# Transposes without a reader in three stages, 256-column token products in the last layer, and one pair of subtractions on another engine

## The chip, the core and the metric

The kernel runs on one core of a Trainium2 chip. The metric is the device time of one execution in microseconds (us); before the change it is 1029.0 us, the median of 3 runs (1028.3 to 1030.1). PE is TensorE, which multiplies matrices; PEld is its loading of the stationary operand, which runs beside the multiplications; DVE is VectorE, ACT is ScalarE, POOL is GpSimd, SP is the engine that issues most of the DMAs.

## The reference, cut to what matters

Two small transformer stacks run one after the other on x, 256 tokens by 1024 channels, in float32. Of the five stages the following is what the change touches:

```python
# first block: a gated mixer, then a feed-forward part
proj = einsum('bsd,dc->bsc', rmsnorm(x, norm_mix_g), w_in)      # 14 groups of 512 columns
...
x = x + einsum('bsd,de->bse', m, w_out)
z = relu(einsum('bsd,df->bsf', rmsnorm(x, norm_ff_g), w_ff1))   # 4096 columns
x = rmsnorm(x + einsum('bsf,fd->bsd', z * z, w_ff2), norm_final_g)
# second block: differential attention + conv_ffn, then latent attention + conv_ffn
u = h @ w_up                                                     # 2 * 2816 columns
c = causal depthwise conv of u + conv_b;  g, val = split(c, 2)
x = x + (silu(g) * val) @ w_down
# after the last conv_ffn: rms_norm(x, final_norm_g)
```

## The kernel before, in words

Every weight is used in two halves. A raw tile of 128 rows and 1024 columns (512 KB) comes from memory on SP's queue, ACT writes its upper half `hi` (L178), DVE the remainder `lo` (L179). Activations have such halves too, written by `halves` (L334 to L337: the upper by ACT, the lower by DVE or by POOL, as the caller asks). A product is then three matmuls in a row, `hi*xh`, `hi*xl`, `lo*xh` (`mm3`, L195); all of them are recorded on L193. `split_to` keeps the weights three units ahead of their use, and loads five raw tiles ahead of that.

`group` computes 512 output columns as four tiles of 128 columns by 256 tokens: for each of 8 values of k there are 4 tiles of 3 matmuls, that is 12 matmuls for a k and 96 for a group, and the moving operand has 256 columns (the tokens). Its argument `between` names functions that run after a given k. `rows` adds 2 to 4 k-tiles to all eight output tiles at once (24 matmuls for each k). The order of the program is the order of the steps; PE executes its matmuls in that order.

Some short work on PE stands between the groups. `stats` gives two functions: `one` sums squares by token (matmuls of 1 column, L295) and `two` spreads the result over the partitions (`bcast`, L320). `gating` in the mixer multiplies 128x128 blocks (L489). In the last conv_ffn alone, `turn_x` transposes the final x: four times, after k = 4, 5, 6 and 7 of group 1, it transposes four 128x128 blocks with the identity (L932). The attention stages transpose too (L761, L807, L1142).

The last conv_ffn writes its result with tokens on the partitions (`last_rows`): the stationary operand is a 128x128 block of the activations and the moving one is 512 columns of a weight, so that a pair of k-tiles is 2 token blocks by 2 halves by 2 k by 3 = 24 matmuls of 512 columns, 264 in all.

In the feed-forward part `z_evac(g)` takes a group of 512 columns from PSUM: scale (DVE, L331), squared relu (DVE, L614), `halves` with POOL for the lower half (L337), in two parts of two tiles. The first one, `z_evac(0)`, is issued after k = 3 of group 1, and the rows of the second matrix that need it come right behind group 1. The program order between 250 and 270 us is: group 0, `one`, k = 0 to 3 of group 1, `two`, `z_evac(0)`, k = 4 to 7 of group 1, `z_evac(1)`, the first rows.

Of the kernel before, what the change touches and what calls it, by code (L numbers as in the profile page):

```python
# [16 lines left out]
P = 128  # L17
T = 256
# [5 lines left out]
HID_T = 22  # L24
# [60 lines left out]
class Builder:  # L85
# [114 lines left out]
    def cols(self, banks, u, n, kk, stride, xh, xl, first, last, tiles=None):  # L200

        for c in tiles if tiles is not None else range(n):
            o = kk * stride + c * P
            self.mm3(banks[c // 2][:, c % 2, :], u.hi[:, o:o + P], u.lo[:, o:o + P], xh, xl,
                     first and c % 2 == 0, last)

    def group(self, units, banks, ncol, xh, xl, nk=KD, between=None, bank=None):

# [206 lines left out]
    def mixer(self):  # L415
        nc, a = self.nc, self.a
# [5 lines left out]
        one, two = self.stats(st)  # L422
# [95 lines left out]
                self.conv(bufs["y"][:, k, :], z[:, i, :], "conv_a", k, 8, None)  # L518
        self.step(r2)
        for j in range(4):  # L520
            self.group(g[4 + j], cb[j], 4, xh, xl, between={4: (lambda j=j: gating(j),)})
            self.step(lambda j=j: cx_evac(j))

        bb = [[], []]
# [75 lines left out]
    def ff(self):  # L600
        nc, a = self.nc, self.a
        w1 = self.weights(a["w_ff1"], 2048, 2)
        w2 = self.weights(a["w_ff2"], 2048, 2)
        xh, xl = lambda k: self.xh[:, k, :], lambda k: self.xl[:, k, :]
        st, z, fb, ob = {}, {}, [[] for _ in range(8)], []
        one, two = self.stats(st)

        def z_evac(g):
            z[g] = (self.b4([4, T], F32R), self.b4([4, T], F32R))
            for i in range(2):  # L610
                sl = slice(2 * i, 2 * i + 2)
                t = self.scaled(fb[g][i], st["r"])
                q = self.t2()
                nc.vector.scalar_tensor_tensor(out=q, in0=t, scalar=0.0, in1=t, op0=ALU.max,  # L614
                                               op1=ALU.mult)
                self.halves(q, z[g][0][:, sl, :], z[g][1][:, sl, :], nc.gpsimd)
        zh, zl = lambda k: z[k // 4][0][:, k % 4, :], lambda k: z[k // 4][1][:, k % 4, :]

        def final(pr, bank):
            if pr == 0:  # L620
                self.norm_in(lambda k: self.gg[:, k:k + 1], lambda k: self.par("g_fin", k))
                p = PAR_AT
                nc.vector.tensor_tensor(self.gg, self.par_sb[:, p["g_fin"]:p["g_fin"] + 8],
                                        self.par_sb[:, p["g_attn0"]:p["g_attn0"] + 8], op=ALU.mult)
            self.residual(pr, bank)
            self.norm_pair(pr)

        def second(g):
            ks = range(4 * g, 4 * g + 4)
            self.row_bank = self.at_bank  # L630
            if g < 7:
                self.rows(w2[4 * g:4 * g + 4], ob, ks, 0, FF_T - 1, zh, zl)
            else:
                self.rows(w2[4 * g:4 * g + 4], ob, ks, 0, FF_T - 1, zh, zl, final)
        for g in range(8):
            if g == 1:
                self.step(one)
            self.group(w1[4 * g:4 * g + 4], fb[g], 4, xh, xl,
                       between={3: (two, lambda: z_evac(0))} if g == 1 else None)
            if g:  # L640
                self.step(lambda g=g: z_evac(g))
                second(g - 1)
        second(7)
# [229 lines left out]
    def conv_ffn(self, i, final=None):  # L873
# [31 lines left out]
        for g in range(11):  # L905
            if g == 1:
                self.step(one)
            bt = {}
            if g == 1:
                bt[3] = (two, lambda: evac(0))  # L910
                if not final:
                    for k in range(4):
                        bt[4 + k] = (lambda k=k: self.turn_x(k // 2, k % 2),)
            self.group(wu[4 * g:4 * g + 4], ub[g], 4, xh, xl, between=bt)
            if g:
                self.step(lambda g=g: evac(g))
            if g >= 2:
                down(g - 2)
# [18 lines left out]
    def last_rows(self, units, banks, ks, xh, xl):  # L937

        def add(b, c):
            ps = banks[2 * b + c].rearrange("p a t -> p (a t)")  # L940
            for u, k in zip(units, ks):
                h, l = xh(k)[:, b * P:(b + 1) * P], xl(k)[:, b * P:(b + 1) * P]
                cs = slice(c * 512, c * 512 + 512)
                self.mm(ps, h, u.hi[:, cs], k == 0, False)
                self.mm(ps, h, u.lo[:, cs], False, False)
                self.mm(ps, l, u.hi[:, cs], False, k == HID_T - 1)

        def fn():
            if not banks:
                banks.extend(self.at_bank() for _ in range(4))  # L950
            for b in range(2):
                for c in range(2):
                    add(b, c)
                    if ks[-1] == HID_T - 1:
                        self.last_piece(b, c, banks[2 * b + c].rearrange("p a t -> p (a t)"))
        self.step(fn, *units)
# [360 lines left out]
```

## Time and profile before

| what | value |
|---|---|
| median of 3 runs | 1029.0 us (1028.3 to 1030.1) |
| profiled execution, its own time | 1023.16 us |
| its span, from the first to the last instruction | 1021.4 us |
| PE busy | 997.7 us, 98% of the span |
| PEld busy | 960.3 us, 94% |
| DVE busy | 745.1 us, 73% |
| ACT busy | 569.7 us, 56% |
| POOL busy | 175.0 us, 17% |
| granted TensorE clock, mean | 0.994 |

The time outside the span is 1.8 us. The profiled execution is one execution, and 5.8 us below the median. A matmul's recorded duration reaches into the next one's, so that its real pace is read from how many start in a stretch of time.

### The profile page before, as it was taken

How to read it: one execution, taken by the hardware profiler on the slowest of the kernel's cores; microseconds unless marked ns; L12 is line 12 of the kernel's file. 1: busy time of each engine (PE TensorE's matmuls, PEld its weight loads, DVE VectorE, ACT ScalarE, POOL GpSimd, SP SyncE). 2: the span in 40 equal slices, each digit the busy share in tenths (PEclk: the TensorE clock that was granted, in tenths of full speed). 3: DMA queues.
4: the chain of work that ended last, by engine and by line, in shares of the span. 5: the costliest groups of instructions: out<-in, count | busy, mean ns of one | idle time of the engine just before them, and what ended most of it. 6: DMA issues, size and time to landing. Idle time of an engine off the chain costs nothing.

```text
span 1021.4 us, 19659 instructions
## 1 busy us (share of the span) xinstructions
PE 997.7 (98%) x7940; PEld 960.3 (94%) x7940; DVE 745.1 (73%) x1124; ACT 569.7 (56%) x895; POOL 175.0 (17%) x121
## 2 busy tenths in 40 slices
PE   8999999999999999989899999999998999999996
PEld 7999999999999999978799999999987899999995
DVE  5667766567656665778868887777889988887774
ACT  6644454445444444846576665555686667655553
POOL 2101300002311221452102201010422121100001
PEclk9999999999999999999999999999999999999999
DMA  9675555554555555353345465555553435655531
GB/s 334 220 259 170 185 184 185 189 187 159 202 196 190 194 194 195 113 206 129 109 159 187 158 209 181 194 181 160 176 168 127 145 114 195 205 190 185 187 104 41
DMA packets 51067, 180.36 MB, mean 177 GB/s; under 512 B 5664, under 2 KB 6176, under 8 KB 50976
## 3 DMA queue, kind: packets, MB, share of 16 engines
q1 hardware_dynamic: 50688, 178.58, 51.9%
q8 instruction: 62, 1.02, 0.4%
q10 hardware_dynamic: 288, 0.52, 0.1%
q14 instruction: 29, 0.24, 0.1%
HBM read 178.04 MB, written 1.05 MB: 175 GB/s over the span
## 4 chain that ended last, share of the span: by engine, by line
PE 88%; DVE 3%; ACT 3%; issue 2%; POOL 2%; DMA 1%; SPq 0%; POOLq 0%; DVEq 0%; ACTq 0%
PE mm L193 60%; PE at L193 24%; DVE lo L179 1%; ACT hi L178 1%; POOL tiny L308 1%; POOL xg L697 1%; DMA raw<-in_w_in 1%; PE at L1119 1%; DVE t L870 1%; PE at L1142 1%; ACT b L741 0%; ACT t L1129 0%; POOL t L869 0%; PE at L489 0%; PE at L1118 0%
## 5 line engine op out<-in xcount | busy, mean ns | idle before, releaser
L193 PE MATMUL mm<-b,hi 128*128 128x256 f32 x3584 | 638.6, 280 | 1.1 <-DVE b L1031 0.8
L193 PEld LDWEIGHTS mm<-b,hi 128*128 128x128 f32 x3584 | 547.9, 188 | 5.1 <-issue 2.1
L179 DVE TENSOR_TENSOR lo<-raw,hi 128x1024 fp32r<-128x1024 f32 (+2 forms) x336 | 416.6, 1251 | 181.9 <-ACT hi L178 180.9
L178 ACT CAST hi<-raw 128x1024 fp32r<-128x1024 f32 (+2 forms) x337 | 345.4, 1037 | 301.5 <-PE mm L193 230.4
L193 PE MATMUL mm<-b,lo 128*128 128x256 f32 x1792 | 499.9, 279 | 0.0
L193 PEld LDWEIGHTS mm<-b,lo 128*128 128x128 f32 x1792 | 336.7, 188 | 0.7 <-issue 0.7
L193 PE MATMUL at<-b,hi 128*128 128x256 f32 x1088 | 190.9, 278 | 1.0 <-POOL b L337 1.0
L193 PEld LDWEIGHTS at<-b,hi 128*128 128x128 f32 x1088 | 165.0, 188 | 2.2 <-POOL b L337 1.2
L193 PE MATMUL at<-b,lo 128*128 128x256 f32 x544 | 151.0, 278 | 0.0
L193 PEld LDWEIGHTS at<-b,lo 128*128 128x128 f32 x544 | 102.0, 187 | 0.0
L894 POOL TENSOR_TENSOR t<-t,t 128x512 f32<-128x512 f32 x22 | 40.3, 1833 | 289.9 <-DVE t L597 251.4
L597 DVE SCALAR_TENSOR_TENSOR t<-t,par,t 128x254 f32<-128x254 f32 (+1 forms) x176 | 76.0, 485 | 11.6 <-ACT t L595 11.0
L280 POOL TENSOR_TENSOR t<-t,t 128x512 f32<-128x512 f32 x18 | 26.0, 1445 | 197.5 <-ACT t L279 196.9
L193 PE MATMUL at<-hi,b 128*128 128x512 f32 x176 | 56.7, 394 | 0.0
L336 ACT CAST b<-t 128x512 fp32r<-128x512 f32 x50 | 30.9, 621 | 43.1 <-POOL t L894 36.4
L331 DVE TENSOR_TENSOR t<-mm,rbc 128x512 f32<-128x512 f32 x76 | 51.6, 687 | 0.2
L337 POOL TENSOR_TENSOR b<-t,b 128x512 fp32r<-128x512 f32 x16 | 29.7, 1864 | 119.6 <-ACT b L336 119.6
L193 PE MATMUL mm<-hi,b 128*128 128x512 f32 x144 | 48.8, 411 | 1.1 <-ACT hi L178 1.1
L595 ACT ACTIVATE t<-t,par 128x256 f32<-128x256 f32 x88 | 46.0, 591 | 6.4 <-DVE t L331 6.4
L337 DVE TENSOR_TENSOR b<-t,b 128x512 fp32r<-128x512 f32 x34 | 24.2, 718 | 23.0 <-ACT b L336 23.0
L193 PEld LDWEIGHTS at<-hi,b 128*128 128x128 f32 x176 | 32.9, 187 | 7.7
L193 PEld LDWEIGHTS mm<-hi,b 128*128 128x128 f32 x144 | 27.8, 194 | 8.2 <-ACT hi L178 1.9
(181 smaller groups left out, 709.2 us busy)
## 6 DMA issues: line engine op xcount, KB each, us to landing
raw<-in_ffn_up SPq DMA_DIRECT2D x88, 512.0 KB, 4.8
raw<-in_w_ff SPq DMA_DIRECT2D x64, 512.0 KB, 4.5
raw<-in_w_in SPq DMA_DIRECT2D x55, 512.0 KB, 4.8
raw<-in_ffn_down SPq DMA_DIRECT2D x44, 512.0 KB, 4.1
raw<-in_da_qk SPq DMA_DIRECT2D x16, 512.0 KB, 4.8
raw<-in_w_proj_a SPq DMA_DIRECT2D x8, 512.0 KB, 4.1
raw<-in_w_proj_b SPq DMA_DIRECT2D x8, 512.0 KB, 3.7
raw<-in_w_out SPq DMA_DIRECT2D x8, 512.0 KB, 4.9
```

The lines of the kernel that those rows point to most:

```text
L178: self.last_hi = self.nc.scalar.copy(hi[:, sl], w[:, sl])
L179: (u.eng or self.nc.vector).tensor_tensor(lo[:, sl], w[:, sl], hi[:, sl].bitcast(F32), op=ALU.subtract)
L193: self.nc.tensor.matmul(out, lhsT, rhs, start=start, stop=stop, skip_group_check=True)
L280: nc.gpsimd.tensor_tensor(self.ss, self.ss, sq, op=ALU.add)
L308: self.nc.gpsimd.tensor_tensor(r, ms, self.mhalf[:, :n], op=ALU.pow)
L331: self.nc.vector.tensor_tensor(o, bank, self.over2(r), op=ALU.mult)
L336: self.nc.scalar.copy(hi, src)
L337: (eng or self.nc.vector).tensor_tensor(lo, src, hi.bitcast(F32), op=ALU.subtract)
L595: nc.scalar.activation(y, z, AF.Identity, scale=w[2], bias=bias)
L597: nc.vector.scalar_tensor_tensor(out=y[:, d:], in0=z[:, :T - d], scalar=w[2 - d], in1=y[:, d:], op0=ALU.mult, op1=ALU.add)
L697: nc.gpsimd.tensor_tensor(xp, xp, self.over2(st["rx"]), op=ALU.mult)
L894: nc.gpsimd.tensor_tensor(y[0], y[0], y[1], op=ALU.mult)
```

## The change

A new function `pulse` takes a bank of the pool `at` and transposes four 128x128 blocks of x into it; nothing reads the bank. It is called twice in each of three places: in the mixer after k = 5 and k = 6 of the fourth of the groups `cb`, in the feed-forward part after k = 4 and k = 5 of group 1, and in the first conv_ffn after k = 4 and k = 5 of group 1. `last_rows` splits each matmul of 512 columns into two of 256. The lower halves of `z_evac(0)` move from POOL to DVE.

```diff
+    def pulse(self):
+
+        ps = self.at_bank().rearrange("p a t -> p (a t)")
+        for i in range(4):
+            self.nc.tensor.transpose(ps[:, i * P:(i + 1) * P], self.x[:, i, 0:P], self.ident)
...
         for j in range(4):
-            self.group(g[4 + j], cb[j], 4, xh, xl, between={4: (lambda j=j: gating(j),)})
+            bt = {4: (lambda j=j: gating(j),)}
+            if j == 3:
+                bt[5] = bt[6] = (self.pulse,)
+            self.group(g[4 + j], cb[j], 4, xh, xl, between=bt)
...
-                self.halves(q, z[g][0][:, sl, :], z[g][1][:, sl, :], nc.gpsimd)
+                self.halves(q, z[g][0][:, sl, :], z[g][1][:, sl, :], nc.gpsimd if g else None)
...
             self.group(w1[4 * g:4 * g + 4], fb[g], 4, xh, xl,
-                       between={3: (two, lambda: z_evac(0))} if g == 1 else None)
+                       between={3: (two, lambda: z_evac(0)), 4: (self.pulse,), 5: (self.pulse,)}
+                       if g == 1 else None)
...
                 if not final:
                     for k in range(4):
                         bt[4 + k] = (lambda k=k: self.turn_x(k // 2, k % 2),)
+                else:
+                    bt[4] = bt[5] = (self.pulse,)
...
-                cs = slice(c * 512, c * 512 + 512)
-                self.mm(ps, h, u.hi[:, cs], k == 0, False)
-                self.mm(ps, h, u.lo[:, cs], False, False)
-                self.mm(ps, l, u.hi[:, cs], False, k == HID_T - 1)
+                for j in range(2):
+                    o = ps[:, j * T:(j + 1) * T]
+                    cs = slice(c * 512 + j * T, c * 512 + (j + 1) * T)
+                    self.mm(o, h, u.hi[:, cs], k == 0 and j == 0, False)
+                    self.mm(o, h, u.lo[:, cs], False, False)
+                    self.mm(o, l, u.hi[:, cs], False, k == HID_T - 1)
```

On PE, in the mixer, the first pulse stands between k = 5 and k = 6 of the fourth group `cb` (its banks are mm_1047 and mm_1048; a row is written as output, then moving operand, then stationary operand; xg holds x):

```order
 L193 MATMUL mm_1048<-b_17_129,hi_1003 128x256
 L193 MATMUL mm_1048<-b_16_128,lo_1004 128x256
+L211 MATMUL at_1144<-ident,xg 128x128 x4
 L193 MATMUL mm_1047<-b_16_128,hi_1043 128x256
 L193 MATMUL mm_1047<-b_17_129,hi_1043 128x256
```

Nothing is moved there; four transposes are put between two triples, and so it is at the five other places.

On PE, in the last conv_ffn, these are the first token products of the row pair that follows group 2, of the kernel before (at_10470 is one of four banks, hi and lo are halves of the activations, b_1542 holds the weight):

```order
L193 MATMUL at_10470<-hi_10347,b_1542_10179 128x512
L193 MATMUL at_10470<-lo_10348,b_1542_10179 128x512
L193 MATMUL at_10470<-hi_10347,b_1542_10179 128x512
L193 MATMUL at_10470<-hi_10377,b_1542_10179 128x512
L193 MATMUL at_10470<-lo_10378,b_1542_10179 128x512
```

and of the change:

```order
L193 MATMUL at_10500<-hi_10586,b_1566_10320 128x256
L193 MATMUL at_10500<-lo_10587,b_1566_10320 128x256
L193 MATMUL at_10500<-hi_10586,b_1566_10320 128x256 x2
L193 MATMUL at_10500<-lo_10587,b_1566_10320 128x256
L193 MATMUL at_10500<-hi_10586,b_1566_10320 128x256
L193 MATMUL at_10500<-hi_10616,b_1566_10320 128x256
```

Each matmul of 512 columns has become two of 256, and each block of the activations is loaded as the stationary operand twice as often.

On DVE, in the feed-forward part, this is `z_evac(0)` and what follows it, of the kernel before (mm_2784 and mm_2785 are the banks of group 0, mm_2916 is one of group 1):

```order
L331 TENSOR_TENSOR t_414_2978<-mm_2784,rbc_2974 128x512
L614 SCALAR_TENSOR_TENSOR t_415_2980<-t_414_2978 128x512
L331 TENSOR_TENSOR t_416_2984<-mm_2785,rbc_2974 128x512
L614 SCALAR_TENSOR_TENSOR t_417_2986<-t_416_2984 128x512
L179 TENSOR_TENSOR lo_3131<-raw_2942,hi_3130 128x1024
L331 TENSOR_TENSOR t_426_3052<-mm_2916,rbc_2974 128x512
```

and of the change (lines 6 to 9 further down; b_415 is the lower half of z):

```order
L337 TENSOR_TENSOR t_416_2988<-mm_2794,rbc_2984 128x512
L623 SCALAR_TENSOR_TENSOR t_417_2990<-t_416_2988 128x512
L337 TENSOR_TENSOR t_418_2994<-mm_2795,rbc_2984 128x512
L343 TENSOR_TENSOR b_415_2987<-t_417_2990,b_414_2986 128x512
L623 SCALAR_TENSOR_TENSOR t_419_2996<-t_418_2994 128x512
L179 TENSOR_TENSOR lo_3151<-raw_2952,hi_3150 128x1024
L343 TENSOR_TENSOR b_415_2987<-t_419_2996,b_414_2986 128x512
L337 TENSOR_TENSOR t_430_3072<-mm_2926,rbc_2984 128x512
```

The two subtractions L343 stand in DVE's queue, each behind a result of ACT that it waits for, and ahead of a weight's lower half and of `z_evac(1)`.

## Rows read from the trace of the kernel before

**Rows 1.** The page's head, its PE row and the granted clock in 40 slices.

```profile
span 1021.4 us, 19659 instructions
PE 997.7 (98%) x7940; PEld 960.3 (94%) x7940; DVE 745.1 (73%) x1124; ACT 569.7 (56%) x895; POOL 175.0 (17%) x121
PEclk9999999999999999999999999999999999999999
```

**Rows 2.** L193 on PE by stretches: start:end, length, busy (matmuls), clock, DMA.

```profile
101.13:252.12 150.99, 150.99 (x1284) 1.00 0.54 180
265.92:417.90 151.98, 151.98 (x1343) 1.00 0.56 187
520.40:522.99 2.59, 2.59 (x24) 1.00 0.80 283
530.89:549.70 18.81, 18.81 (x168) 1.00 0.39 127
550.39:555.80 5.41, 5.41 (x48) 1.00 0.96 331
558.60:734.32 175.72, 175.72 (x1494) 1.00 0.53 176
850.77:861.43 10.66, 10.66 (x97) 1.00 0.30 91
867.02:878.32 11.30, 11.30 (x97) 1.00 0.58 181
985.37:996.67 11.30, 11.30 (x97) 1.00 0.01 1
```

**Rows 3.** Timeline of PE at the first turn_x: start, length, engine, line, tiles, count.

```profile
844.57 0.28 PE L193 MATMUL mm<-b,lo 128*128 128x256 f32 x1
844.68 0.60 PE L932 MATMUL at<-ident,xg 128*128 128x128 f32 x4
845.04 0.48 PE L193 MATMUL mm<-b,hi 128*128 128x256 f32 x2
845.35 0.28 PE L193 MATMUL mm<-b,lo 128*128 128x256 f32 x1
```

**Rows 4.** L932 by form: shortest, median and longest duration in ns.

```profile
L932 PE MATMUL at<-ident,xg x16: 271/272/273, 844.7 to 850.4; 128*128 128x128 f32 x16
```

**Rows 5.** Timeline of PE, two other short pieces: attention's transposes, conv_ffn's sums.

```profile
519.51 0.82 PE L761 MATMUL at<-ident,b 128*128 128x128 f32 x6
...
549.70 0.50 PE L295 MATMUL at<-ones,t 128*128 128x1 f32 x4
```

**Rows 6.** Timeline of PE where the feed-forward part's first rows begin.

```profile
264.19 0.28 PE L193 MATMUL mm<-b,lo 128*128 128x256 f32 x1
264.30 0.28 PE L193 MATMUL at<-b,hi 128*128 128x256 f32 x1
265.59 0.38 PE L193 MATMUL at<-b,hi 128*128 128x256 f32 x1 [1.00 <-POOL b L337]
```

**Rows 7.** Timelines of DVE, ACT and POOL around z_evac(0).

```profile
261.24 0.69 DVE L614 SCALAR_TENSOR_TENSOR t<-t 128x512 f32<-128x512 f32 x1
263.18 1.22 DVE L179 TENSOR_TENSOR lo<-raw,hi 128x1024 fp32r<-128x1024 f32 x1
...
262.56 1.35 ACT L336 CAST b<-t 128x512 fp32r<-128x512 f32 x2
...
263.25 6.23 POOL L337 TENSOR_TENSOR b<-t,b 128x512 fp32r<-128x512 f32 x3 [9.65 <-ACT b L336]
```

**Rows 8.** L193 on PE by stretches of 512-column matmuls alone, columns as above.

```profile
878.32:883.93 5.61, 5.61 (x27) 1.00 0.91 314
417.90:429.09 11.19, 11.19 (x50) 1.00 0.27 88
```

**Rows 9.** All engines by stretches: PE, PEld, DVE, ACT, POOL busy, then clock and DMA.

```profile
265.92:417.90 151.98, 151.98 (x1343) 151.98 (x1342) 93.27 (x89) 70.63 (x84) 29.63 (x17) 1.00 0.56 187
558.60:734.32 175.72, 175.72 (x1495) 175.72 (x1494) 136.19 (x195) 103.71 (x143) 32.60 (x17) 1.00 0.53 176
867.02:996.67 129.65, 129.65 (x937) 121.86 (x936) 103.51 (x134) 71.44 (x92) 10.39 (x8) 1.00 0.53 174
```

## The prediction

> **What bounds the kernel now.** I read the head of the page first: PE is busy for 997.7 of 1021.4 us at a granted clock of 0.9 or more in every slice [rows 1]. So PE is the bound nearly everywhere, and the question is not who makes it wait but how fast its matmuls follow one another. A matmul's duration can't tell that, since it overlaps the next; the count of starts can. So the second view is that of L193 on PE by stretches, with the 256-column matmuls alone [rows 2]. A count there includes one to three matmuls that only reach over an edge; in the long stretches this is nothing. The mixer from 101.13 us: 1282 starts in 150.99 us, 117.8 ns each. The feed-forward part from 265.92 us: 1341 starts in 151.98 us, 113.3 ns each. The first conv_ffn from 558.60: 1492 in 175.72 us, 117.8 again. The operation, its shape and the granted clock (1.00, so the upper of the two levels, 2.4 GHz) are the same in all three. There are two paces, 4.45 ns apart, and a stretch keeps its pace for up to 1500 matmuls.
>
> **What switches the pace.** The changes of pace that I found in the rows all lie at an interruption of the stream. Feed-forward: PE waits 1.00 us for POOL, 264.30 to 265.59 [rows 6], and the fast pace begins behind that wait; it goes on through the 512-column matmuls at 417.90. Last conv_ffn: four transposes at 844.68 [rows 3]; triples start 0.35 us apart before them, 0.34 after, and from 850.77 the rows show 94 in 10.66 us, 113.4 each [rows 2]. Then come the first 512-column products, and from 867.02 on each group of 96 takes 11.30 us, 117.7 each, up to the last at 985.37 [rows 2]. Not every interruption helps: after six transposes in the attention at 519.51 [rows 5] the pace stays slow (22 in 2.59 us from 520.40), and the sums by token at 549.70 [rows 5] turn a fast stream (166 in 18.81 us before) into a slow one (46 in 5.41 us after) [rows 2]. I read this as two stable spacings between the load of the stationary operand and the matmul behind it: an interruption draws one, and an undisturbed stream keeps it. That is an inference; the paces themselves are rows.
>
> **The pulses: price.** A pulse is turn_x without its copy, so its price is a row. From the `lo` at 844.57 to the `lo` at 845.35 are 0.78 us, with three matmuls and four transposes; three matmuls alone take 0.35. A pulse costs 0.43 us, 109 ns a transpose, and six cost 2.6 us [rows 3]. The record of one transpose is 272 ns long [rows 4], but four end to end start 0.36 us before the next matmul, so most of it overlaps. The Trainium skill, "TensorE: Matmul & The Clock Gate", section "Part 4: PE-mode transpose", puts a transpose at about 275 ns in one kernel's context; that is the recorded duration here, and 24 of them would by that estimate cost 6.6 us in place of 2.6. The trace's starts decide, so I take 2.6. Nothing reads the banks and x, the identity and the banks are long ready, so a pulse should wait for nothing; the banks that it takes from the pool of four were emptied before.
>
> **The pulses: what they bring, if the pace becomes the fast one.** Mixer: 1284 matmuls of 256 columns stand between the last gating and the next sums (36 of the fourth group, eleven groups' worth 1056, 192 of rows), 1260 of them behind the second pulse: 1260 x 4.45 = 5.6 us, less 0.9 for two pulses, 4.7 us. First conv_ffn: 48 of group 1, nine groups (864), 528 of rows and 72 of the next stage, less the 24 ahead of the second pulse: 1488 x 4.45 = 6.6, less 0.9, 5.7 us. Feed-forward: it runs fast already in this execution, so the pulses bring 24 x 4.45 = 0.1 us and cost 0.9.
>
> **z_evac(0) on DVE.** The wait of 1.00 us costs 1.29 - 0.12 = 1.17 us from start to start [rows 6]. What was late is POOL's lower half: 263.25 to about 265.1, one third of 6.23 us [rows 7]. On DVE it takes 0.7 (the like-sized L614, 0.69) behind ACT's upper half, which is ready at 263.2, so about 264.0. PE reaches the rows 0.9 us later than before because of the pulses, at 265.1. The wait goes: 1.2 us gained, and feed-forward comes to 1.2 + 0.1 - 0.9 = 0.4 us. Next in line is DVE itself: it gets 1.4 us more work, and stands 0.6 us or so at ACT's result, ahead of a weight half that ended at 264.4 and would end near 266 [rows 7]. The rows use it one k later, 265.1 + 2.7 = 267.8, so it is covered; the half behind `z_evac(1)` has less cover, an estimated 0.6 us from the same durations. If that is wrong PE waits up to 1 us; I take none.
>
> **256-column token products.** At 512 columns the price is 5.61 us for 24, 233.8 ns, and 11.19 for 48, 233.1 [rows 8]: 233.3. Two of 256 cost 226.7 at the fast pace and 235.6 at the slow one, so 264 of them bring 1.8 us or cost 0.6. What matters more is what stands between them: after the four turn_x the stream is fast and the 512-column products end that [rows 2]. Without them the eight groups from 867.02 on would stay fast: 768 x 4.45 = 3.4 us. Together 5.2 us. Twice as many loads of the stationary operand fit: every 256-column stream in the kernel has one for each matmul.
>
> A rule speaks against this edit. The Trainium skill, same page, section "Back-to-back issue gap", makes an isolated matmul N / 2.4 + 2.5 ns at the full clock, by which 256 columns take 109.2 and 512 take 215.8: one pace alone, and two halves would cost 2.5 ns more than the whole, 264 x 2.5 = 0.7 us lost. The rows differ from it at both widths (113.3 or 117.8, and 233.3).
>
> **Sum.** 4.7 + 0.4 + 5.7 + 5.2 = 16.0 us off the profiled execution's 1023.2: 1007.2. Its 1023.2 is 5.8 us below the median of 1029.0. One reading: in the timed runs the wait on POOL left feed-forward at the slow pace, 1341 x 4.45 = 6.0 us more. With that the pulses there gain these 6.0 too and the timed result is 1007. The other: the 5.8 us have another cause and stay, 1013. The trace can't decide, and I put down 1010, between them.
>
> **Can the others follow?** At 4% more pace DVE goes from 136.2 of 175.7 us (78%) to 81% in the first conv_ffn, from 103.5 of 129.7 (80%) to 83% in the last; ACT and the DMAs stand lower, and feed-forward has kept the fast pace at the same weight traffic with 187 GB/s [rows 9].
>
> **Rivals.**
> (1) One of mixer, first conv_ffn or last conv_ffn does not turn or stay fast. For: the transposes at 519.51 did not turn the pace, and the token form has never been seen at 256 columns. It costs back 5.6 to 6.6 us (5.8 in the last): 1013 by the profile, up to 1019 with the median's offset. Chance 0.27.
> (2) Two or more fail: 1019 to 1025. Chance 0.12.
> (3) Slower: a pulse leaves the pace as it is, and the wait whose end made feed-forward fast is gone. The pulses cost 2.6 us, the end of the wait gives 1.2, the token halves at the slow pace cost 0.6, and feed-forward loses its 6.0: 1023.2 + 8.0 = 1031.2, 2.2 over the median (and 1037 if the median's 5.8 have another cause). It decides where fewer than about 450 matmuls gain the fast pace, since the edits cost 2.0 us net without it (2.0 / 0.00445). Against it: the four turn_x at 844.68 are the same four transposes behind the same 12 matmuls after the same `bcast` as in the first conv_ffn, and the pace turned there [rows 3]. Chance 0.08. By the one pace for each width in the skill's section the pulses would be mere cost too; the two paces of the rows speak against that.
> (4) The pace turns but DVE or the weights can't follow, waits appear and undo the pace: 1014 to 1020. Against it [rows 9]. Chance 0.08.
> The forecast has 0.45.
>
> **Range and chances.** Both readings of the median and case (1) reach from 1005 to 1019; (2) adds 1025 with small weight. 1004 to 1021 leaves out less than 2 in 10. The likeliest case alone is 1005 to 1014. About 0.2% (2 us) is what a measurement of this kernel can tell from no change. Faster: the forecast, (1), (2), (4) less a little, 0.87; same 0.06; slower 0.07, from (3).
>
> **What would show it.** L193 by stretches: the mixer behind the second pulse, feed-forward, first conv_ffn and all groups of the last at 113.3 ns; a stage at 117.8 is a pulse that failed. Each pulse at 0.43 us. No wait of PE for POOL before the first rows, and none for DVE soon after. I am wrong if the stages stay at 117.8, if they lose the pace half way, or if the timed runs differ from the profile by more than 6 us.

## The result, and the profile after

The kernel with the change takes **1014.46 us** (median of 4 runs, 1012.61 to 1015.79); the kernel before took 1028.65 beside it (4 runs, 1023.5 to 1030.1). The ratio on record is 0.9884, 95% interval 0.9845 to 0.9923 (the two medians alone give 0.9862). The forecast was 1010.0 with a range of 1004 to 1021. The profiled execution of the change is the one of 1012.61 us, 10.6 below the profiled execution of before.

The page's head, its PE row and the granted clock of the change, which answer to [rows 1]:

```profile
span 1010.8 us, 20230 instructions
PE 986.3 (98%) x8228; PEld 961.3 (95%) x8228; DVE 745.2 (74%) x1126; ACT 568.9 (56%) x895; POOL 169.7 (17%) x119
PEclk9999999999999999999999999999999999999999
```

PE has 288 matmuls more and is busy 11.4 us less; its share of the span is the same 98%. PE was the bound and still is, and its work got shorter though there is more of it. Where, the count of starts tells. L193 on PE by stretches of the change, columns as in [rows 2]:

```profile
104.39:247.28 142.89, 142.89 (x1260) 1.00 0.57 185
257.39:412.52 155.13, 155.13 (x1368) 1.00 0.57 187
554.66:723.39 168.73, 168.73 (x1488) 1.00 0.56 181
757.34:761.38 4.04, 1.49 (x9) 0.58 0.39 116
841.20:852.16 10.96, 10.96 (x96) 1.00 0.31 98
852.16:869.36 17.20, 17.20 (x148) 1.00 0.64 210
869.36:885.46 16.10, 16.10 (x144) 1.00 0.70 222
885.46:902.55 17.09, 17.09 (x148) 1.00 0.58 193
985.36:1002.48 17.12, 17.12 (x146) 1.00 0.01 1
```

The first three rows are the stages behind the pulses of the mixer, the feed-forward part and the first conv_ffn: 142.89 / 1260, 155.13 / 1368 and 168.73 / 1488 are 113.4 ns each. The mixer and the first conv_ffn ran at 117.8 before [rows 2]. The rows from 841.20 on are the last conv_ffn, and there the pace is not what was forecast: fast for its first 96 matmuls, then slow for 146, fast for 142 to 144, slow again, and so to the end (a row's count takes in two or three matmuls that only reach over an edge; starts alone give 117.85 ns where it is slow and 113.36 where it is fast). Every piece begins at the first token products of a pair and ends ahead of the next pair's. The pace changes at all nine steps from a group to token products, and at none of the eight steps from token products back to a group.

The same from stage to stage, as the time to the end of each in the profiled executions, before and after: sums of the mixer 252.12 and 247.28 (-4.84); end of feed-forward's rows 417.90 and 412.52 (-0.54 more); sums of the attention 549.70 and 544.55 (+0.23); sums of the first conv_ffn 734.32 and 723.39 (-5.78); end of the latent attention 836.74 and 827.47 (+1.66); end of the span 1021.37 and 1010.82 (-1.28). Together -10.55.

The +0.23 of the attention hides two terms that nearly cancel: about 350 of its matmuls ran at 113.3 ns before and at 117.8 in the change (+1.6), and only the profile before has a piece at the lower clock there, which is the row at 453.36 below (-1.5: from the end of the wait ahead of it, the first 20 matmuls take 3.81 us before and 2.27 in the change).

The +1.66 is the row at 757.34: a granted clock of 0.58 in 4.04 us, which is a piece at the lower of the two levels, 1.2 GHz. PE had waited 1.74 us for DVE just ahead of it. In the profile of before the same thing lies elsewhere, at 453.36, behind a wait of 2.2 us of PE for DVE:

```profile
453.36:456.77 3.41, 3.41 (x17) 0.50 0.73 253
```

17 matmuls in 3.41 us would take about 2.0 at 117.8 ns each. Over the 14 profiles of this study there are none to two such pieces in the body of the kernel, all behind one of three waits of PE in the two attention stages. The wait of 1.74 us stands in all 14 (the profile before has it too, 1.75 us ahead of 768.14, and no lower clock behind it), and ten have a piece behind it. The kernel of the change, run again below, has the piece at 437 us that this profile lacks. So I take these pieces for no part of the change; that the change doesn't make the one at 757 us likelier is not shown, since the three profiles without 256-column token products all lack it.

### The profile page after: what moved, and what is told of

Same layout as the page of the kernel before. It is cut to its first block, busy times and chain, and to the rows that moved or that the text cites. A ratio compares the mean times of both kernels' runs of the same rounds, so it can differ in the third digit from the quotient of the medians.

```text
span 1010.8 us, 20230 instructions
## 1 busy us (share of the span) xinstructions
PE 986.3 (98%) x8228; PEld 961.3 (95%) x8228; DVE 745.2 (74%) x1126; ACT 568.9 (56%) x895; POOL 169.7 (17%) x119
## 4 chain that ended last, share of the span: by engine, by line
PE 86%; DVE 4%; ACT 3%; POOL 3%; issue 2%; DMA 1%; SPq 0%; POOLq 0%; DVEq 0%; ACTq 0%
PE mm L193 58%; PE at L193 24%; DMA raw<-in_w_in 1%; DVE lo L179 1%; DVE t L880 1%; ACT hi L178 1%; PE at L1133 1%; POOL tiny L314 1%; POOL xg L707 1%; ACT b L751 1%; PE at L1156 1%; POOL t L879 1%; POOL t L286 0%; ACT t L1143 0%; PE at L495 0%
## 5 line engine op out<-in xcount | busy, mean ns | idle before, releaser
L193 PE MATMUL mm<-b,hi 128*128 128x256 f32 x3584 | 629.3, 279 | 1.1 <-DVE b L1045 0.8
L193 PEld LDWEIGHTS mm<-b,hi 128*128 128x128 f32 x3584 | 543.7, 188 | 4.0 <-issue 1.8
L193 PE MATMUL mm<-b,lo 128*128 128x256 f32 x1792 | 497.9, 278 | 0.0
L193 PEld LDWEIGHTS mm<-b,lo 128*128 128x128 f32 x1792 | 336.4, 188 | 0.7 <-issue 0.7
L193 PE MATMUL at<-b,hi 128*128 128x256 f32 x1088 | 187.5, 277 | 0.0
L193 PEld LDWEIGHTS at<-b,hi 128*128 128x128 f32 x1088 | 164.1, 188 | 1.1 <-issue 1.0
L193 PE MATMUL at<-b,lo 128*128 128x256 f32 x544 | 150.4, 276 | 0.0
L193 PEld LDWEIGHTS at<-b,lo 128*128 128x128 f32 x544 | 102.2, 188 | 0.0
L193 PE MATMUL at<-hi,b 128*128 128x256 f32 x352 | 62.9, 279 | 0.0
L193 PEld LDWEIGHTS at<-hi,b 128*128 128x128 f32 x352 | 54.5, 189 | 0.0
L193 PE MATMUL at<-lo,b 128*128 128x256 f32 x176 | 49.2, 279 | 0.0
L193 PE MATMUL mm<-hi,b 128*128 128x512 f32 x144 | 47.6, 402 | 1.6 <-ACT hi L178 1.6
L343 POOL TENSOR_TENSOR b<-t,b 128x512 fp32r<-128x512 f32 x14 | 25.8, 1840 | 123.0 <-ACT b L342 123.0
L343 DVE TENSOR_TENSOR b<-t,b 128x512 fp32r<-128x512 f32 x36 | 25.6, 716 | 22.9 <-ACT b L342 22.8
```

The lines of the kernel that those rows point to most:

```text
L193: self.nc.tensor.matmul(out, lhsT, rhs, start=start, stop=stop, skip_group_check=True)
L343: (eng or self.nc.vector).tensor_tensor(lo, src, hi.bitcast(F32), op=ALU.subtract)
```

## The experiments

Four theories were to be told apart: (T) four transposes in a row turn the pace of the matmuls behind them, and that is the gain; (R1) the gain comes from the 256-column tokens or from the lower halves on DVE; (R2) any interruption or any extra work would do; (R3) a pulse draws the pace at random.

**The three parts alone.** The kernel before with the pulses only, with the 256-column tokens only, and with the lower halves on DVE only.

```diff
 e1 = before +   def pulse(self): ...
                 bt[5] = bt[6] = (self.pulse,)          (mixer, j == 3)
                 4: (self.pulse,), 5: (self.pulse,)     (feed-forward, g == 1)
                 bt[4] = bt[5] = (self.pulse,)          (conv_ffn, final)
 e2 = before +   for j in range(2): ... self.mm(o, h, u.hi[:, cs], k == 0 and j == 0, False)
 e3 = before +   self.halves(q, ..., nc.gpsimd if g else None)
```

> The kernel before with the six pulses alone; the last layer's products stay at 512 columns, POOL keeps the lower halves. Theory (a pulse turns the stream to the spacing of 113.3 ns, which then lasts): mixer behind the pulses, feed-forward and first conv_ffn at 113.3 to 113.4 ns a matmul, last conv_ffn at 117.8 as before; 10 to 11 us under a profile of the kernel before whose feed-forward is fast, that is 1011 to 1014 us in the profile and about the same in the timed runs. Rival (the time came from the other two edits): no stage but feed-forward differs from before, and six pulses cost 2.6 us: 1025 to 1032.

Measured: 1013.18 us (4 runs, 1011.01 to 1018.3) against 1028.75 of before (19 runs, 1027.38 to 1031.86), ratio 0.9856, interval 0.9826 to 0.9886. L193 by stretches in e1, the mixer, feed-forward and the first conv_ffn behind their pulses:

```profile
104.50:247.50 143.00, 142.80 (x1261) 1.00 0.55 185
257.50:412.00 154.50, 154.50 (x1365) 1.00 0.55 187
554.00:722.00 168.00, 168.00 (x1485) 1.00 0.54 180
```

The three stages run at the fast pace, the groups of the last conv_ffn at the slow one as before, and from the last turn_x to the last matmul PE takes 162.81 us, to the hundredth what it took before. POOL still writes the lower halves of `z_evac(0)` here, and PE doesn't wait for them: from the sums of the mixer to the end of feed-forward's rows e1 takes 165.23 us, the change 165.24.

> The kernel before with the 256-column token products alone. In the profile of the change the last conv_ffn changed its pace at the first token product of each row pair, from fast to slow and from slow to fast by turns. Theory (the step from a group to token products switches the spacing, whatever stands ahead of the last layer): the same alternation, about 145 matmuls at 117.8 and 143 at 113.4, and the last conv_ffn is 1.5 to 2.5 us shorter than before. Rival (the alternation comes from how the stream arrives from the earlier stages): one pace throughout, a gain of 5.2 us or a loss of 0.6.

Measured: 1028.24 us (10 runs), ratio 0.9994, interval 0.9982 to 1.0006. The alternation is the same as in the whole change, with a turn at each of the nine steps to token products, 161.04 us from the last turn_x to the last matmul and 8.62 us behind it; the feed-forward part ran at the slow pace in the profile.

> The kernel before with the lower halves of the first z on DVE alone. Theory (the wait of 1.0 us for POOL is what turned feed-forward to the fast spacing): without the wait feed-forward stays at 117.8 ns, so it gives 1.2 us and loses 6.0: 1027 to 1029 in the profile. Rival (feed-forward is fast for another reason, for example its shapes): 113.3 without the wait and 1021 to 1023.

Measured: 1028.25 us (10 runs), ratio 0.9998, interval 0.9987 to 1.0009. PE no longer waits for POOL ahead of feed-forward's rows.

What follows: the pulses bring everything that can be measured; R1 is out. The profiles of e2 and e3 also bear on the 5.8 us between the profile of before and its median. Timeline of PE in e2, where the first rows of feed-forward begin, and L193 by stretches behind it:

```profile
264.09 0.28 PE L193 MATMUL at<-b,hi 128*128 128x256 f32 x1
265.38 0.38 PE L193 MATMUL at<-b,hi 128*128 128x256 f32 x1 [1.01 <-POOL b L337]
...
266.06:422.00 155.94, 155.94 (x1326) 1.00 0.55 181
```

L193 by stretches in e3, which has no wait there:

```profile
259.06:420.00 160.94, 160.94 (x1369) 1.00 0.54 184
```

The wait of e2 is that of [rows 6], 1.01 us in place of 1.00, and behind it stand 155.94 / 1326 = 117.6 ns (117.8 by starts alone; so it is with each 117.6 below): the slow pace, where the profile of before had 113.3. So the same wait left one pace in one execution and the other in another. Without the wait (e3) the stage is slow too, 117.6. Of the 48 times of the kernel before that stand beside the change and these runs, five lie between 1022.0 and 1024.3 (four of them among the seven beside e5 to e8) and one at 1025.3, all others at 1027.4 or more. The profile of before, at 1023.16, is one of the low ones; that the low times are those with a fast feed-forward part is inferred from the two profiles, since no other time of that kernel was profiled.

**One pulse in place of two** in each stage, to see whether the second does anything.

```diff
-                bt[5] = bt[6] = (self.pulse,)
+                bt[5] = (self.pulse,)
```

> The change with the first pulse of each stage alone. Theory (the first pulse already turns the spacing, the second only keeps it): all three stages at 113.3 ns, 3 x 0.43 = 1.3 us less than the change: 1011.3 in a profile like that of the change, 1013 median. Rival (two are needed, or each is a draw): at least one stage at 117.8, 5 to 6 us more for each.

Measured: 1014.62 us (4 runs, 1010.12 to 1015.73), ratio 0.9855, interval 0.9829 to 0.988. One pulse turned feed-forward and the first conv_ffn; in the mixer it failed. L193 by stretches, the mixer of e4:

```profile
102.61:252.30 149.69, 149.69 (x1272) 1.00 0.54 180
```

That is 117.7 each. A pulse in the mixer can fail (R3 for this stage), and since two pulses fail there too in runs below, e4 doesn't show that two are needed.

**Is it the transposes?** Four plain matmuls of the same operands in the place of the four transposes (the identity and x change sides, without the transpose mode), and one transpose in the place of four; both twice in each stage.

```diff
-            self.nc.tensor.transpose(ps[:, i * P:(i + 1) * P], self.x[:, i, 0:P], self.ident)
+            self.nc.tensor.matmul(ps[:, i * P:(i + 1) * P], self.ident, self.x[:, i, 0:P],
+                                  start=True, stop=True)                              (e5)
-        for i in range(4):
+        for i in range(1):                                                             (e6)
```

> The change with each pulse's four transposes replaced by four plain float32 matmuls of the same blocks (same reads, same bank, about 0.9 us a pulse from the gating's 8 records at 0.11). Theory (a transpose sets the spacing, an ordinary short product does not: behind the gating's plain products the stream was slow four times of four): the three stages stay at 117.8 ns. Rival (any interruption of this kind turns it): they run at 113.3 as in the change.

Measured: 1032.14 us, one run (the kernel before beside e5 to e8: median 1024.27, 7 runs, 1021.99 to 1031.1). L193 by stretches, the three stages of e5:

```profile
105.50:253.50 148.00, 148.00 (x1259) 1.00 0.55 179
265.00:420.00 155.00, 155.00 (x1318) 1.00 0.57 184
568.00:736.00 168.00, 168.00 (x1429) 1.00 0.55 179
```

All three at 117.6: an interruption of 0.9 us (each plain matmul leaves two records, eight for a pulse) turned nothing. The edit changes the kind of the pulse and its length at once, and the last experiment shows that the length alone can matter; plain matmuls in another number were not tried.

> The change with one transpose in each pulse in place of four. Theory (the spacing after the transposes decides, and one has it already): 113.3 ns in the three stages, and a pulse costs about 0.1 us. Rival (it takes several in a row to settle): at least two stages at 117.8, as behind single transposes in the latent attention before.

Measured: 1022.13 us, one run. L193 by stretches in e6, and the one row of its timeline that tells why the second stage is fast all the same:

```profile
105.20:253.50 148.30, 148.24 (x1259) 1.00 0.55 180
266.44:420.00 153.56, 153.56 (x1349) 1.00 0.56 186
560.20:736.00 175.80, 175.60 (x1492) 1.00 0.55 176
...
266.21 0.19 PEld L193 LDWEIGHTS at<-b,hi 128*128 128x128 f32 x1 [0.21 <-DVE b L343]
```

Mixer and first conv_ffn are at 117.8. Feed-forward was slow behind its single transposes, then PE's load waited 0.21 us for the lower half of z that DVE makes, and behind that wait the stage is fast. So R2 is out for single transposes and for eight records of plain matmuls, each in one execution; a wait may turn the pace as well.

**The last conv_ffn.** If the pace turns each time that PE goes from a group to token products, an odd number of such turns between two groups leaves every second group slow. The seventh experiment splits the products of a pair: a quarter behind the group, the rest behind the first k of the next group, so that there are two such turns for each group.

```diff
+            if rest:
+                bt[0] = (rest,)
             self.group(wu[4 * g:4 * g + 4], ub[g], 4, xh, xl, between=bt)
...
-                down(g - 2)
+                rest = down(g - 2)
...
+        self.step(some(pieces[:1]), *units)
+        return some(pieces[1:])
```

> The change with each row pair of the last layer, up to the eighth, in two parts: the first quarter (12 matmuls) behind the group as now, the other three quarters behind k = 0 of the next group (12 matmuls later). Theory (each step from a group to token products switches the pace): the pace switches twice for a group, so about 24 matmuls of 144 run slow and 120 fast or the reverse; starting fast, the last conv_ffn is 1.5 to 2.5 us shorter than in the change. Rival (the pace alternates by the period of a row pair, whatever the steps): no gain.

Measured: 1010.19 us, one run. L193 by stretches in e7, two periods and the end:

```profile
854.45:867.94 13.49, 13.49 (x121) 1.00 0.49 158
867.94:870.79 2.85, 2.85 (x27) 1.00 0.79 227
870.90:884.40 13.50, 13.50 (x122) 1.00 0.65 222
982.95:999.80 16.85, 16.85 (x146) 1.00 0.00 1
```

By starts, 118 or 119 of each 144 matmuls run at 113.36 and 25 or 26 at 118.1; from the last turn_x to the last matmul there are 159.41 us, 1.63 less than in the change. The pace turns at each beginning of token products, 17 of 17.

**The end.** The change's last matmul starts 1.77 us earlier after the last turn_x than before (162.81 and 161.04 us), but the end behind it grew from 8.13 to 8.62 us. DVE's timeline at the end of the change:

```profile
1001.11 0.69 DVE L976 TENSOR_TENSOR b<-at,b 128x512 f32<-128x512 f32 x1
1001.72 0.15 DVE L986 SCALAR_TENSOR_TENSOR tiny<-lsq 128x1 f32<-128x1 f32 x1
1001.78 0.69 DVE L989 TENSOR_TENSOR b<-b,b 128x512 f32<-128x512 f32 x1
1002.91 0.49 DVE L993 TENSOR_SCALAR b<-b,tiny 128x512 f32<-128x512 f32 x1 [0.44 <-POOL tiny L314]
1003.31 0.15 DVE L982 TENSOR_SCALAR lsq<-lsq 128x1 f32<-128x1 f32 x1
1003.37 0.68 DVE L983 TENSOR_TENSOR b<-b,b 128x512 f32<-128x512 f32 x1
1003.97 0.68 DVE L976 TENSOR_TENSOR b<-at,b 128x512 f32<-128x512 f32 x1
```

and at the end of the kernel before, where the same lines are L962, L972, L975, L979, L968 and L969:

```profile
1012.27 0.69 DVE L962 TENSOR_TENSOR b<-at,b 128x512 f32<-128x512 f32 x1
1012.88 0.15 DVE L972 SCALAR_TENSOR_TENSOR tiny<-lsq 128x1 f32<-128x1 f32 x1
1012.95 0.69 DVE L975 TENSOR_TENSOR b<-b,b 128x512 f32<-128x512 f32 x1
1013.67 0.69 DVE L962 TENSOR_TENSOR b<-at,b 128x512 f32<-128x512 f32 x1
1014.28 0.48 DVE L979 TENSOR_SCALAR b<-b,tiny 128x512 f32<-128x512 f32 x1
```

Before, the addition of the last piece (L962) stands ahead of the scaling that waits for POOL's rsqrt, and runs 0.43 us after the start of the last matmul (1013.24). In the change it stands behind that scaling and two more, and runs 1.77 after it (1002.20). The eighth experiment gives the last pair alone its 512 columns back.

```diff
-                for j in range(2):
-                    o = ps[:, j * T:(j + 1) * T]
-                    cs = slice(c * 512 + j * T, c * 512 + (j + 1) * T)
+                n = 1 if ks[-1] == HID_T - 1 else 2
+                w = 512 // n
+                for j in range(n):
+                    o = ps[:, j * w:(j + 1) * w]
+                    cs = slice(c * 512 + j * w, c * 512 + (j + 1) * w)
```

> The change with 512-column products kept in the last row pair alone, 24 of 264. In the change DVE's queue has the last piece's addition behind three instructions of the other token block, one of which waits for POOL; with this edit it stands ahead of them, as in the kernel before. Theory (that order made the end 0.5 us longer): from the last matmul's start to the end of the span 8.1 us as before in place of 8.6, and nothing else changes on PE but 24 x (233.3 - 2 x 117.8) = under 0.1 us. Rival (the end is longer because of the narrower products themselves): 8.4 to 8.6 us.

Measured: 1011.49 us (6 runs, 1009.72 to 1017.18), ratio on record 0.9843, interval 0.9795 to 0.9891 (the two medians alone give 0.9875). DVE's timeline at its end, and L193 in its mixer:

```profile
1007.70 0.69 DVE L978 TENSOR_TENSOR b<-at,b 128x512 f32<-128x512 f32 x1
1008.30 0.48 DVE L995 TENSOR_SCALAR b<-b,tiny 128x512 f32<-128x512 f32 x1
...
104.30:252.50 148.20, 148.20 (x1260) 1.00 0.55 179
```

The addition is ahead of the scaling again, 0.44 us after the start of the last matmul (1007.26), and the end is 8.14 us as before the change. The edit gives back the width and the order together, so the run alone doesn't part the theory from its rival; for the order speaks the trace of the change, where DVE stands idle for 0.44 us ahead of the scaling, from 1002.47 on, when the last matmul (0.28 us from 1002.20) is just done and the addition could have run. The mixer's two pulses both failed in this profile (117.6).

**Both mends, a third pulse, and the change again,** on one chip.

```diff
 e9  = the change + the edits of e7 and e8
 e10 = e9 +  bt[5] = bt[6] = bt[7] = (self.pulse,)      (mixer)
 e11 = the change, unaltered
```

> The change with both mends in the last conv_ffn: row pairs up to the eighth in two parts, and 512 columns in the last pair. Theory (each mend acts on its own term, so they add): from the last turn_x to the last matmul 159.2 to 159.5 us, the end behind the last matmul 8.1 to 8.2, together 2.1 us less than the change has; the median then lies 1.5 to 2.5 us below that of the change in this call, near 1011 if the mixer turns about as often as it did, and 15 to 18 below the kernel before. Rival (the mends share a cause, so that one of them uses the other up, for example because the wide pair runs in the pace that the split rows leave): the two together bring 1.6 us or less, and the median differs from the change's by less than 1 us.

Measured: 1014.59 us (5 runs, 1013.27 to 1015.32), ratio to before 0.9858, interval 0.9839 to 0.9877. From the last turn_x to the last matmul 159.25 us and an end of 8.14: 2.27 less than the change, so each mend brings its own part. The median is only 0.97 below that of the change beside it (e11), where 1.5 to 2.5 were expected and the rival had less than 1. The mixer doesn't explain it, as it was slow in both profiles (148.1 us for 1260 here). The profile of e9 is 1.41 us shorter than that of e11: it gains the 2.27, and reaches the last turn_x 0.86 later, lost in the attention stages. Five times each, which spread over 2 and 5.5 us, can't part the two by the median; the pieces of the last conv_ffn in the trace do.

> The kernel with both mends and a third pulse in the mixer, one k after the second. Theory (each pulse draws a pace for the stream behind it, and once fast the stream stays fast): a third draw makes the slow mixer rarer; the mixer runs at 113.3 in the profile, and of ten or so times at most two lie 4 us or more above the lowest; the median is 0 to 3 us below that of the kernel with two pulses. Rival (what decides is fixed ahead of the pulses, for example by how the stream reached them, so a third pulse changes nothing): the same share of high times as with two pulses, and 0.4 us more for the third. Second rival (a pulse can also turn a fast stream slow): the profile shows a change of pace between the pulses, and no fewer high times.

Measured: 1013.17 us (1009.76, 1013.53, 1008.84, 1013.17, 1015.17), ratio 0.9836, interval 0.9811 to 0.9862. The mixer of the profile is fast, behind the first pulse already. The times spread as before: a third pulse like the others doesn't make the slow mixer rarer as far as five times tell. The two medians differ by less than their runs spread.

> The change itself, unaltered, in the same call, for a direct comparison and for the spread of its times. Theory (the mixer's pulses are a draw): its times fall into two groups some 5 us apart, about 1010 to 1012 and 1014 to 1018, with a median of 1011 to 1016; the profile has 113.3 behind the pulses of feed-forward and first conv_ffn in either case, and 117.8 or 113.3 in the mixer according to the group that its time belongs to. Rival (the spread has another cause, the drops of the granted clock alone): steps of 1.7 us for each drop, and a mixer at 113.3 also in a time of the higher group.

Measured: 1015.56 us (1016.74, 1012.03, 1014.97, 1015.56, 1017.5), ratio 0.9868, interval 0.9846 to 0.989; before 1029.48 (9 runs). L193 by stretches in e11, the mixer and feed-forward:

```profile
104.50:252.50 148.00, 148.00 (x1259) 1.00 0.55 179
262.90:418.00 155.10, 155.10 (x1369) 1.00 0.56 186
```

The same kernel has 117.6 ns here in its mixer, where the first profile of it had 113.4. So whether the mixer turns is settled anew in each execution: R3 holds for this stage. The times don't fall into two clean groups, though; the pieces at the lower clock (two in this profile, some 1.4 to 1.7 us each) would blur them, which is an estimate.

Over the eight profiles with pulses of four transposes, feed-forward and the first conv_ffn were fast in all eight; the mixer in four. Within one mixer all pulses did the same: in the change, e1, e7 and e10 the first turned the pace and those behind it left it fast, in e8, e9 and e11 both failed, as did the one pulse of e4. That asks for pulses that aren't alike.

**Pulses of unlike length** in the mixer of the mended kernel: four, five and six transposes.

```diff
-                bt[5] = bt[6] = bt[7] = (self.pulse,)
+                for q in (4, 5, 6):
+                    bt[1 + q] = (lambda q=q: self.pulse(q),)
```

> The kernel with both mends and three pulses of unlike length in the mixer: four, five and six transposes, where the kernel with the third pulse has three of four. Theory (in the slow cases like pulses meet the stream alike, in the profiles all of a mixer's pulses turned it or none; pulses of unlike length meet it differently): the mixer is at 113.3 in the profile behind one of the pulses at the latest; four of five times or more lie within 3 us of the lowest, and the median is 1009 to 1011. Rival (the outcome is fixed before the pulses, whatever their length): times from 1009 to 1016 as with three like pulses, a median of 1013 to 1015, and in the profile either all pulses turn it or none.

Measured: 1011.43 us (1015.2, 1015.41, 1010.51, 1011.43, 1009.67), ratio 0.9834, interval 0.9813 to 0.9855. PE's timeline at the three pulses of the profiled execution, then L193 behind each:

```profile
101.72 0.60 PE L212 MATMUL at<-ident,xg 128*128 128x128 f32 x4
...
103.58 0.71 PE L212 MATMUL at<-ident,xg 128*128 128x128 f32 x5
...
105.49 0.82 PE L212 MATMUL at<-ident,xg 128*128 128x128 f32 x6
...
102.39:103.57 1.18, 1.18 (x12) 1.00 0.70 257
104.35:105.48 1.13, 1.13 (x12) 1.00 0.00 0
106.38:252.90 146.52, 146.52 (x1246) 1.00 0.54 180
```

The four failed (12 matmuls in 1.18 us), the five turned the stream fast (12 in 1.13), and the six turned it slow again, for the 1247 behind it. The first half of the theory held: pulses of unlike length meet the stream differently. The second half fell, since the last pulse undid the gain: a pulse can also turn a fast stream slow; three of the five times lie within 3 us of the lowest. In the trace's own records a matmul starts 110 ns after its load begins at the fast pace, 115 or 116 at the slow one.

One reading, which no run shows, is that the transposes, the step from group to tokens and a wait all act alike: they place the next matmul anew against the load ahead of it, and which pace comes of it depends on where it was. The outcome stands in the records before the stream goes on: from the start of the last matmul ahead of a pulse of four to the first one behind it the 22 pulses that turned a slow stream took 473 or 474 ns, the eight that failed 475 to 478. So what decides in the mixer lies in the pulse or ahead of it; what it is stays open. Leaving out the six, so that a mixer gets a four and a five, is the obvious next kernel, and wasn't tried; in an execution where the four works, the five might undo it.

## Why the prediction was right, and where its sum was off

**Mechanism.** Two stable paces, an undisturbed stream keeps its pace, four transposes turn it: e1, with e5 and e6 as counter-tests, shows this for feed-forward and the first conv_ffn, and in the mixer it held in four of the eight profiles with such pulses. The inference that an interruption draws a spacing between load and matmul agrees with the records (110 against 115 ns), but is not shown to be the cause.

**Terms.** Mixer, forecast -4.7: -4.84 in the profile. Feed-forward, -0.4: -0.54, with no wait for POOL or DVE; the cover for DVE's lower half held here and was short by 0.21 us in e6. But the 1.2 us that the sum credits to the move to DVE are not its work: e1 without the move is as fast there. The pulses, which bring PE to the rows 0.9 us later, are enough, as POOL's half is ready at about that time (by [rows 7] at 263.25 + 6.23 / 3 = 265.3, not the prediction's 265.1). First conv_ffn, -5.7: -5.78. The price of a pulse, 0.43: 0.44 by the starts in the change, from the `lo` at 102.11 to the `lo` at 102.90, less the 0.35 of three matmuls. PE's timeline there:

```profile
102.11 0.28 PE L193 MATMUL mm<-b,lo 128*128 128x256 f32 x1
102.23 0.60 PE L211 MATMUL at<-ident,xg 128*128 128x128 f32 x4
102.59 0.48 PE L193 MATMUL mm<-b,hi 128*128 128x256 f32 x2
102.90 0.28 PE L193 MATMUL mm<-b,lo 128*128 128x256 f32 x1
```

**The term that was mis-sized: the last conv_ffn,** forecast -5.2, measured -1.28. It consisted of 3.4 for eight groups that "would stay fast" and 1.8 for two halves in place of a whole. The step that failed is "the 512-column products end that. Without them the eight groups from 867.02 on would stay fast".

The fast pace ends at the first token products at 256 columns too, so the width is not what ended it. The beginning of token products, which have the hidden rows stationary and the weights moving (in the rows ahead of the prediction that show them, hi and lo are the halves of the weight and b holds the hidden rows), turns the pace at 256 columns each time, from fast to slow and from slow to fast; at 512 columns the one stream at 113.3 ns fell to 117.8 and those at 117.8 kept it.

So four of the eight groups were fast, an estimated 384 x 4.45 = 1.7 us of the 3.4, and of the halves 192 ran fast and 336 slow, which by the prediction's own prices brings 0.2 of the 1.8. Measured is a gain of 1.77 us on PE. By its own sign, "if they lose the pace half way", the prediction was wrong in this stage. e7, with two such turns for each group, moved 1.63 us more. The other 0.49 was overlooked: the order of DVE's instructions at the end, which stands in the program ahead of any run; e8 shows the 0.49 to be the price of the narrow products in the last pair.

The Trainium skill, "TensorE: Matmul & The Clock Gate", section "Back-to-back issue gap", gives an isolated matmul at the full clock one gap for each width, and by that estimate this edit would have lost 0.7 us. By e2 it gained 1.77 us on PE and lost 0.49 behind it, so neither that estimate nor the forecast's sum gives the number.

**The median.** The profile's sum was -16.0 and came to -10.55: 3.9 short in the last conv_ffn, 1.66 for the piece at the lower clock, 0.23 in the attention, 0.4 gained over the forecast in the other three. Reading one fits e2 and the 48 times: the runs of before mostly have feed-forward slow, 6.0 us. From the profiles, 10.55 + 6.0 = 16.6 for an execution whose mixer turns, about 5.5 less for one whose mixer doesn't; 14.2 between the medians lies between. That the median is inside the range is in part luck: the forecast of 1010 had counted half of those 6.0 us, and the other half, 3 us, made up for part of what the last conv_ffn, the lower clock and the mixers that didn't turn took away.

**Rivals.** Rival (1), one stage doesn't turn or stay fast, is what happened in the last conv_ffn in part, and in the mixer in about half the executions; its 1013 to 1019 holds the median. The forecast's own 1005 to 1014 misses it by half a microsecond. Rival (3) put a failed pulse at a loss; only e5, where nothing turned and the pulses cost twice as much, came out there, at 1032.14. In the change PE waits neither for DVE nor for a weight in the stretches behind the pulses, so rival (4) had no part.

## What to carry to other kernels

Where one engine is busy for 98%, count the starts in long stretches before you believe that it can't go faster: the same instruction may have two paces, and 4% lay between them here. A cheap interruption of the right kind can turn the pace, but it can turn it back too, so put it where nothing follows that turns it again, and take several profiles of the same kernel, since one shows only what that execution drew. When an edit makes work finer at the very end, look at the order of the engines behind it first: 0.5 us of a gain of 1.8 went there.

## What the runs showed of the hardware that was not expected

A stream of one load and one 256-column matmul keeps either 113.3 or 117.8 ns for up to 1500 matmuls, at a granted clock of 1.00 in both. Four transposes turned it 16 times out of 16 in two stages and in four profiles of eight in a third; five and six in a row turned it in opposite directions in one execution; eight records of plain matmuls didn't, in three stages of one execution. Each step from a group (weights stationary) to 256-column token products (hidden rows stationary) changed the pace, in nine such steps of nine in the change's last conv_ffn and 17 of 17 in e7; the step back from token products to a group changed it in none. A granted clock at the lower level for 3.41 us came behind waits of PE of 1.7 to 2.2 us, but in some executions and not in others: the profiles of one kernel had one piece (the change) and two (e11).
